# Splitting the hidden activations of an MLP group inside the up group ahead of their down products, and not during another group's down products

## The chip, the cores and the metric

The kernel runs on one core of a Trainium2 chip. The metric is the device time of one execution in microseconds (us). A core has five engines that take their instructions independently: TensorE (PE in the profile; its weight loads are PEld), VectorE (DVE), ScalarE (ACT), GpSimd (POOL) and SyncE (SP), the last of which only issues DMAs here.

## The reference

One layer of a streaming encoder on a float32 sequence of 512 frames with 1024 features:

```python
h = h + concat([fox_attention(...), hgrn2(...)]) @ w_out
h = h + memory_cross_attention(rmsnorm(h, norm_x_g), mem_n, w_xq, w_xkv, w_xo)
u = rmsnorm(h, norm_ff_g) @ w1            # w1: 1024 x 4096
h = h + jnp.square(jax.nn.relu(u)) @ w2   # w2: 4096 x 1024
return rmsnorm(h, final_norm_g)
```

The change lies in the last two products, the squared-ReLU MLP.

## The kernel before

**Precision by splitting.** TensorE multiplies in a reduced float32 format. To keep the precision, each operand is split in two: a high half (ACT copies the float32 data into the reduced format) and a low half (DVE subtracts the high half from the data). A product is then three matmuls: high by high, high by low, low by high. For weights this is `split_of` (lines 178 to 189): ACT at line 182 writes `whu` or `whd` (up or down weight), DVE at line 186 writes `wlu` or `wld`. For the hidden activations, the squared ReLU of the up products, it is `hidden_part` (lines 1491 to 1501): ACT at line 1496 writes the high half of `hb`, DVE at line 1498 or 1500 the low half. One `hb` is 128 x 512 numbers in each half.

**Groups and products.** The 4096 hidden features are cut into eight groups of 512. Groups 2 to 7 compute their up product in seven block products instead of eight (a Strassen-like scheme, `mlp_up7`), and all groups do so for the down product (`mlp_down`). The seven products are named "1", "5", "6", "2", "7", "3", "4", in the order in which TensorE does them (`PRODUCTS`). Each needs its own combination of weight blocks (some added up in DRAM ahead of time by accumulating DMAs on the POOL queue, line 446, or added into a loaded block, line 1359) and of activation blocks. The activation combinations of a group are formed by `hidden_sums` on DVE (lines 1481 to 1484) after its up products: `n6`, `s5`, `s7`, `s3`, besides plain quarters of the squared activations `sq`. In the profile, an `hb` made from a combination reads `hb<-s` (keys "5", "7", "3") or `hb<-n` (key "6"), and one made from a plain quarter `hb<-sq` (keys "1", "2", "4").

**Order of the groups.** The main loop (lines 1698 to 1707) does up group 1, and then for each further group g: up group g, `hidden_sums(g)`, down group g-1. So the sequence is up 1, down 0, up 2, down 1, ... up 6, down 5, up 7, and at the end the down products of groups 6 and 7 together, alternating. When a down group g-1 runs, the activations of group g are already there.

**Where the hb splits are written.** `hb_order` lists all keys in the order of use. `hidden_ahead(key, n)` splits the next n keys from `key` on that are not split yet and whose group has been summed. It is called

- in the up loop (line 1700), after each of the seven products of an up group, for the down group that follows. The count is 0 after the first product, then 1, 2, 3 and 4;
- in `mlp_down`, ahead of each product for its own key (line 1538), and after each product for four keys from its own on (`HB` is 4, line 1562). The four keys may reach into the next group.

In the kernel before, the calls at line 1562 after products "7", "3" and "4" of a down group thus split keys "1", "5" and "6" of the following group. In the up group between, only key "2" is left to split.

**Weights.** The seven up weights of a group are prepared in the order "1", "6", "5", "2", "7", "3", "4" (`SPLITS`), the down weights in the order of use. `unit` (lines 1374 to 1386) keeps the splits about four weights ahead of the product in hand and the loads (line 1345, on the SP queue) about eight. High and low halves rotate through four buffers each.

**Buffers.** The pool `s4` has 12 buffers of 4 KB per partition. Four hold the result rows `acc` throughout the MLP. The other eight are shared by the `hb` and by part of the raw weights (the "6" block, which is later turned into "4", and two of each five others).

**What sets the order.** TensorE's order is the program's, by hand (line 332). For ACT, DVE, POOL and SP a planner orders the instructions when the kernel is built: it runs a model of the engines, and whenever an engine is free in it, it gives it the ready instruction that comes first in program order. An instruction whose output needs a buffer is ready only when one is free in the model. Weight splits count as written 20 instructions later than they are (`ahead(PW)`, line 1353), except those of up weights "3" and "4". So a split can run well ahead of its place in the program, if an engine and a buffer are free.

In an up group, ACT also copies product "1" from bank U to bank V (line 1426), product "5" from bank Y (line 1429) and the sum with "6" from U to Y (line 1431), and does the squared ReLU (lines 1389, 1390). TensorE may go on into a bank only after such a copy out of it. In a down group DVE adds the finished products to `acc` (lines 1513, 1515).

Of the kernel before, what the change touches and what calls it, by code (L numbers as in the profile page):

```python
# [40 lines left out]
RAWS, HB, LOADS = 5, 4, 8  # L41
# [5 lines left out]
def emit(  # L47
# [69 lines left out]
    def mm(name, shape=(S,)):  # L117
        return mmp.tile([P] + list(shape), F32, tag="mm", name=name)
# [1191 lines left out]
    sqs, comb, hbs = {}, {}, {}  # L1310
# [63 lines left out]
    def unit(*key):  # L1374

        while key not in units:
            unit_q.popleft()[1]()
        got = units[key]
        at = order.index(key)
        if key[0] == "u" and key[2] in ("5", "6"):  # L1380
            at = at - 1 if key[2] == "5" else at
        while unit_q and len(order) - len(unit_q) < at + 4:
            unit_q.popleft()[1]()
        while load_q and len(order) - len(load_q) < at + LOADS:
            load_q.popleft()()
        return got
# [104 lines left out]
    def hidden_part(g, name):  # L1491

        src = comb[g][name]
        hb = s4([2, 2, HS], f"hb{g}{name}", R)
        sign = -1.0 if name == "6" else 1.0
        ac.activation(hb[:, 0], src, AF.Copy, scale=sign)  # L1496
        if name == "6":
            ve.scalar_tensor_tensor(hb[:, 1], src, -1.0, f(hb[:, 0]), op0=ALU.mult, op1=ALU.subtract)
        else:
            ve.tensor_tensor(hb[:, 1], src, f(hb[:, 0]), ALU.subtract)  # L1500
        hbs[g, name] = hb

    def hidden_ahead(key, n):

        used = hb_order.index(key)
        for k in hb_order[used : used + n]:
            if k not in hbs and k[0] in comb:
                hidden_part(*k)

    def add_to(ps, rows, half, t, sign):  # L1510
        a = acc[2 * rows + t][:, half * S : (half + 1) * S]
        if sign > 0:
            ve.tensor_tensor(a, ps, a, ALU.add)
        else:
            ve.scalar_tensor_tensor(a, ps, -1.0, a, op0=ALU.mult, op1=ALU.add)
# [11 lines left out]
    def mlp_down(gs):  # L1527

        end = gs[-1] == NG - 1
        banks = {}  # L1530
        for n, name in enumerate(PRODUCTS):
            bank, first_, goes = PLAN[name]
            if end and name == PRODUCTS[-1]:
                last_product(gs, banks)
                return
            for g, t in [(g, t) for g in gs for t in range(2)]:
                whi, wlo = unit("d", g, name)
                hidden_ahead((g, name), 1)
                hb = hbs[g, name]
                if first_ and g == gs[0]:  # L1540
                    banks[bank, t] = {"U": sc, "Y": tr}[bank](f"{bank}{g}{t}")
                ps = banks[bank, t]
                ts_ = slice(t * P, (t + 1) * P)
                for k in range(2):
                    hi, lo = hb[:, 0, k, ts_], hb[:, 1, k, ts_]
                    begin = first_ and g == gs[0] and k == 0
                    te.matmul(ps, hi, whi[:, k, :], start=begin, stop=False, skip_group_check=True)  # L1547
                    te.matmul(ps, hi, wlo[:, k, :], start=False, stop=False, skip_group_check=True)  # L1548
                    at = te.matmul(ps, lo, whi[:, k, :], start=False, stop=k == 1, skip_group_check=True)  # L1549
                presum.tick(6 * S / 2400, at)  # L1550
                if end and (g, t) == (gs[0], 1):
                    hidden_ahead((g, name), HB + 1)
                if g != gs[-1]:
                    continue
                if name == "1":
                    banks["V", t] = mm(f"V{g}{t}")
                    ac.activation(banks["V", t], ps, AF.Copy)
                for rows, half, sign in goes:
                    add_to(ps, rows, half, t, sign)
                    if end and (name, rows) in FINAL:  # L1560
                        finish(2 * rows + t, half)
            hidden_ahead((gs[-1], name), HB)
            yield

    def last_product(gs, banks):
# [68 lines left out]
    def finish(tb, half):  # L1634

        a = acc[tb]
        cs = slice(half * S, (half + 1) * S)
        if tb not in fin:
            e = sm(1, f"fe{tb}")
            ac.activation(t2(f"fj{tb}"), a[:, cs], AF.Square, scale=1.0 / 32.0, accum_out=e)  # L1640
            gp.tensor_tensor(e, e, eps3[:, tb : tb + 1], op=ALU.add)
            ag = t2(f"fa{tb}")
            gp.tensor_tensor(ag, a[:, cs], gfin[half], op=ALU.mult)
            fin[tb] = (e, cs, ag)
            return
        o = s4([D], f"fo{tb}")
        r = row_scale(squares(tb, o, cs, fin[tb][0], f"fv{tb}"), f"fr{tb}")
        if tb == 1:

            deferred.extend((tb, half, o, r))  # L1650
            return
        scale_a(tb, o, r)
        dma_a(tb, o)
        scale_b(tb, half, o, r, gfin[half])
# [43 lines left out]
    for g in range(1, NG):  # L1698
        for n, _ in enumerate(mlp_up_group(g)):
            hidden_ahead((g - 1, PRODUCTS[0]), min(n, HB))  # L1700
            if g == 1:
                next(sums, None)
                next(sums, None)
        hidden_sums(g)
        if g < NG - 1:
            for _ in mlp_down((g - 1,)):
                pass
# [4 lines left out]
    for _ in mlp_down((NG - 2, NG - 1)):  # L1712
        pass
# [28 lines left out]
```

## Time and profile before

| | |
|---|---|
| median of 3 runs | 761.94 us |
| lowest and highest | 761.64 and 762.18 us |
| the profiled execution, whole time | 762.01 us |
| its span, first to last instruction | 760.1 us |
| TensorE matmuls busy | 747.9 us (98% of the span) |
| VectorE busy | 540.1 us (71%) |
| ScalarE busy | 430.7 us (57%) |
| granted TensorE clock, mean | 0.997 |

The profile comes from one execution. Times in a timeline count from the start of the span. A line of it gives start, duration, engine, line of the kernel, operation, tile written <- tiles read, and shapes; in brackets stand the idle time of the engine just before and the instruction that ended it. Consecutive instructions overlap at their ends, so the distance between two starts can be shorter than a duration. A line of waits gives who waited for whom, the sum in us, how often, and the longest. Tile names carry no group number; which group an `hb` or a weight belongs to follows from the order. L1547 to L1549 are the three matmuls of a down product, L1420 to L1422 those of an up product.

### The profile page before, as it was taken

The page shows a single profiled execution, that of the slowest core. Times are in us where ns is not written, and L with a number is a line of the kernel's source. Part 1 is how long each engine was busy: PE and PEld are TensorE (multiplying, and loading weights), DVE is VectorE, ACT ScalarE, POOL GpSimd, SP SyncE. Part 2 cuts the span into 40 slices and gives each one's busy share as a digit, 9 for nine tenths or more (in the row PEclk, how much of TensorE's full clock was granted, in tenths as well). Part 3 has the DMA queues.
Part 4 walks back from the last instruction along what each step waited for, and adds up shares of the span by engine and source line. Part 5 has one row for each costly group of instructions (what it writes and reads, how often), then busy time and mean ns, then how long its engine had stood idle before and what let it go on. Part 6 is the DMA issues. An engine that isn't in the chain of part 4 may idle for free.

```text
span 760.1 us, 12027 instructions
## 1 busy us (share of the span) xinstructions
PE 747.9 (98%) x4501; PEld 648.8 (85%) x4501; DVE 540.1 (71%) x844; ACT 430.7 (57%) x715; POOL 197.3 (26%) x274
## 2 busy tenths in 40 slices
PE   9999999999999999999999999999999999999996
PEld 6889888888888988788888888898989889898985
DVE  5647863677778667755536658968787777878697
ACT  5655554656666533244434395667575757474873
POOL 7207431323442236621111100111111111100034
PEclk9999999999999999999999999999999999999998
DMA  8641987567946688966659849797988888967452
GB/s 248 195 118 57 321 254 230 179 226 242 329 157 217 215 189 189 193 139 137 129 131 180 182 93 269 165 267 190 235 235 208 216 240 212 233 195 225 135 112 110
DMA packets 106619, 148.17 MB, mean 195 GB/s; under 512 B 6033, under 2 KB 73146, under 8 KB 106562
## 3 DMA queue, kind: packets, MB, share of 16 engines
q1 hardware_dynamic: 83826, 109.12, 44.0%
q0 software_dynamic: 22144, 37.25, 28.0%
q10 hardware_dynamic: 592, 1.05, 0.4%
q8 instruction: 35, 0.57, 0.3%
q14 instruction: 22, 0.18, 0.1%
HBM read 143.19 MB, written 48.25 MB: 252 GB/s over the span
## 4 chain that ended last, share of the span: by engine, by line
PE 92%; DVE 3%; ACT 1%; issue 1%; DMA 1%; POOL 1%; SPq 0%; ACTq 0%; POOLq 0%
PE U L1547 4%; PE U L1548 4%; PE U L1549 4%; PE uU L1420 3%; PE uU L1421 3%; PE uU L1422 3%; PE wo L255 2%; PE xw L255 2%; PE xw L257 2%; PE xw L256 2%; PE u L257 2%; PE wo L256 2%; PE u L255 2%; PE Y L1547 2%; PE Y L1549 2%; PE Y L1548 2%
## 5 line engine op out<-in xcount | busy, mean ns | idle before, releaser
L186 DVE TENSOR_TENSOR wld<-wrd,whd 128x1024 fp32r<-128x1024 f32 x56 | 68.3, 1222 | 15.8 <-ACT whd L182 15.7
L182 ACT ACTIVATE whd<-wrd 128x1024 fp32r<-128x1024 f32 x56 | 59.1, 1055 | 17.6 <-PE uU L1421 6.8
L186 DVE TENSOR_TENSOR wlu<-wru,whu 128x1024 fp32r<-128x1024 f32 x42 | 49.7, 1218 | 24.5 <-ACT whu L182 24.5
L182 ACT ACTIVATE whu<-wru 128x1024 fp32r<-128x1024 f32 x42 | 43.6, 1054 | 25.4 <-PE U L1549 11.1
L1547 PE MATMUL U<-whd,hb 128*128 128x512 f32 x120 | 46.8, 390 | 0.0
L1548 PE MATMUL U<-wld,hb 128*128 128x512 f32 x120 | 46.8, 390 | 0.0
L1549 PE MATMUL U<-whd,hb 128*128 128x512 f32 x120 | 46.7, 389 | 0.0
L446 POOL DMA_DIRECT2D wsd<-in_w_dram x16 | 17.5, 1093 | 80.3 <-PE xw L257 18.3
L1016 POOL TENSOR_SCALAR bi<-nF,Ft 128x128 f32<-128x128 f32 (+3 forms) x32 | 21.2, 670 | 59.8 <-PE pt L1048 34.7
L446 POOL DMA_DIRECT2D wsu<-in_w_dram x12 | 14.1, 1176 | 65.9 <-PE xq L257 21.0
L1422 PE MATMUL uY<-xs_hi,wlu 128*128 128x256 f32 x96 | 27.8, 290 | 3.2 <-DVE wlu L186 3.1
L1359 POOL DMA_DIRECT2D wru<-in_w_dram x6 | 7.9, 1314 | 88.3 <-DVE wlu L186 88.3
L1359 POOL DMA_DIRECT2D wrd<-in_w_dram x8 | 9.7, 1210 | 80.0 <-DVE wld L186 63.3
L1496 ACT ACTIVATE hb<-sq 128x512 fp32r<-128x512 f32 x24 | 15.1, 631 | 24.4 <-DVE wlu L186 8.3
L1422 PE MATMUL uU<-x_hi,wlu 128*128 128x256 f32 x96 | 27.2, 283 | 0.0
L1420 PE MATMUL uU<-xs_hi,whu 128*128 128x256 f32 x96 | 27.2, 283 | 0.0
L1421 PE MATMUL uU<-xs_lo,whu 128*128 128x256 f32 x96 | 27.2, 283 | 0.0
L1422 PE MATMUL uU<-xs_hi,wlu 128*128 128x256 f32 x96 | 27.2, 283 | 0.0
L1421 PE MATMUL uU<-x_lo,whu 128*128 128x256 f32 x96 | 27.2, 283 | 0.0
L1420 PE MATMUL uY<-xs_hi,whu 128*128 128x256 f32 x96 | 27.1, 283 | 0.0
L1420 PE MATMUL uU<-x_hi,whu 128*128 128x256 f32 x96 | 27.1, 283 | 0.0
L1421 PE MATMUL uY<-xs_lo,whu 128*128 128x256 f32 x96 | 27.1, 283 | 0.0
(997 smaller groups left out, 2685.0 us busy)
## 6 DMA issues: line engine op xcount, KB each, us to landing
wsd<-in_w_dram SPq DMA_DIRECT2D x24, 512.0 KB, 5.6
wrd<-in_w_dram SPq DMA_DIRECT2D x24, 512.0 KB, 6.0
wrd<-wsd SPq DMA_DIRECT2D x24, 512.0 KB, 4.1
wsu<-in_w_dram SPq DMA_DIRECT2D x18, 512.0 KB, 7.7
wru<-in_w_dram SPq DMA_DIRECT2D x18, 512.0 KB, 7.6
wru<-wsu SPq DMA_DIRECT2D x18, 512.0 KB, 5.1
wsd<-in_w_dram POOLq DMA_DIRECT2D x16, 512.0 KB, 8.0
wsu<-in_w_dram POOLq DMA_DIRECT2D x12, 512.0 KB, 6.8
```

The lines of the kernel that those rows point to most:

```text
L182: at = ac.activation(hi, raw, AF.Copy)
L186: ve.tensor_tensor(lo, raw, f(hi), ALU.subtract)
L255: te.matmul(ps, wh, hi, start=n_ == 0 and not begun, stop=False)
L256: te.matmul(ps, wh, lo, start=False, stop=False)
L257: at = te.matmul(ps, wl, hi, start=False, stop=k == order[-1])
L446: yield gp.dma_start(wsum[kind, g, name], src, accum_op=ALU.add, **more)
L1420: te.matmul(ps[:, i, :], whi[:, k, ws], xh[:, k, :], start=begin, stop=False, skip_group_check=True)
L1421: te.matmul(ps[:, i, :], whi[:, k, ws], xl[:, k, :], start=False, stop=False, skip_group_check=True)
L1422: at = te.matmul(ps[:, i, :], wlo[:, k, ws], xh[:, k, :], start=False, stop=k == UK - 1, skip_group_check=True)
L1547: te.matmul(ps, hi, whi[:, k, :], start=begin, stop=False, skip_group_check=True)
L1548: te.matmul(ps, hi, wlo[:, k, :], start=False, stop=False, skip_group_check=True)
L1549: at = te.matmul(ps, lo, whi[:, k, :], start=False, stop=k == 1, skip_group_check=True)
```

## The change

`hidden_ahead` gets a third argument, the groups within which it may split ahead. The call behind each down product passes the groups whose down products are running, so it no longer reaches into the next group. The calls in the up loop, which pass nothing, are unchanged, and now find keys "1", "5" and "6" not yet split. They split "1" after up product "5", "5" after "6", "6" after "2", and "2" after "7". For group 6, whose keys alternate with those of group 7, they split "1" after "5" and "5" after "2". Every `hb` is computed from the same numbers as before, and none is added or left out.

```diff
-    def hidden_ahead(key, n):
+    def hidden_ahead(key, n, within=None):
 
         used = hb_order.index(key)
         for k in hb_order[used : used + n]:
-            if k not in hbs and k[0] in comb:
+            if k not in hbs and k[0] in comb and (within is None or k[0] in within):
                 hidden_part(*k)
...
-            hidden_ahead((gs[-1], name), HB)
+            hidden_ahead((gs[-1], name), HB, gs)
             yield
```

## The prediction

> **What bounds the kernel now.** I read the page first, then TensorE's waits from the start of the MLP on, then the stretches around each wait on TensorE, VectorE (DVE) and ScalarE (ACT). Two lines of the page, and the only line of the waits view of TensorE from 440 us to the end:
>
> ```profile
> span 760.1 us, 12027 instructions
> PE 747.9 (98%) x4501; PEld 648.8 (85%) x4501; DVE 540.1 (71%) x844; ACT 430.7 (57%) x715; POOL 197.3 (26%) x274
> ...
> PE uY L1422 <- DVE wlu L186: 3.1, 5, 0.7
> ```
>
> TensorE is busy nearly throughout, so only its few gaps can be won or widened. In the MLP one thing makes it wait: the low half of an up weight (wlu) for product "5", the second product of an up group. The timeline of TensorE at that place, one stretch for each up group from 2 to 7 (start, duration; in brackets the idle time before it and what ended it):
>
> ```profile
> 497.36 0.28 PE L1421 MATMUL uY<-xs_lo,whu 128*128 128x256 f32 x1
> 497.94 0.38 PE L1422 MATMUL uY<-xs_hi,wlu 128*128 128x256 f32 x1 [0.30 <-DVE wlu L186]
> 498.16 0.28 PE L1420 MATMUL uY<-xs_hi,whu 128*128 128x256 f32 x1
> 498.28 0.28 PE L1421 MATMUL uY<-xs_lo,whu 128*128 128x256 f32 x1
> ...
> 537.14 0.28 PE L1421 MATMUL uY<-xs_lo,whu 128*128 128x256 f32 x1
> 538.12 0.39 PE L1422 MATMUL uY<-xs_hi,wlu 128*128 128x256 f32 x1 [0.70 <-DVE wlu L186]
> 538.34 0.28 PE L1420 MATMUL uY<-xs_hi,whu 128*128 128x256 f32 x1
> ...
> 578.30 0.39 PE L1422 MATMUL uY<-xs_hi,wlu 128*128 128x256 f32 x1 [0.71 <-DVE wlu L186]
> ...
> 618.49 0.39 PE L1422 MATMUL uY<-xs_hi,wlu 128*128 128x256 f32 x1 [0.70 <-DVE wlu L186]
> ...
> 658.67 0.39 PE L1422 MATMUL uY<-xs_hi,wlu 128*128 128x256 f32 x1 [0.71 <-DVE wlu L186]
> ...
> 697.87 0.28 PE L1421 MATMUL uY<-xs_lo,whu 128*128 128x256 f32 x1
> 698.25 0.39 PE L1422 MATMUL uY<-xs_hi,wlu 128*128 128x256 f32 x1
> 698.47 0.28 PE L1420 MATMUL uY<-xs_hi,whu 128*128 128x256 f32 x1
> ```
>
> These matmuls normally follow each other every 0.12 us (498.16 to 498.28). From the one before the late one to the one after it should take 0.24 us. It takes 0.80 in group 2, a loss of 0.56; 1.20 in group 3, a loss of 0.96; 0.60 in group 7, a loss of 0.36. The loss is the bracketed idle time plus 0.26, so groups 4, 5 and 6 lose 0.97, 0.96 and 0.97. Together **4.78 us**, more than the 3.1 of the waits view.
>
> Why is wlu late? The DVE timeline through the end of the down group before up group 3 and into that group, the chain of waits there, and DVE's busy time by stretch (the columns of the last are stretch, length, then busy time and instructions of PE, PEld, DVE, ACT and POOL, clock, DMA share, GB/s):
>
> ```profile
> 530.38 0.68 DVE L1500 TENSOR_TENSOR hb<-sq,hb 128x512 fp32r<-128x512 f32 x1
> 530.98 1.22 DVE L186 TENSOR_TENSOR wlu<-wru,whu 128x1024 fp32r<-128x1024 f32 x1
> ...
> 533.32 0.68 DVE L1500 TENSOR_TENSOR hb<-s,hb 128x512 fp32r<-128x512 f32 x1
> 533.91 1.22 DVE L186 TENSOR_TENSOR wlu<-wru,whu 128x1024 fp32r<-128x1024 f32 x1
> 535.05 1.28 DVE L1513 TENSOR_TENSOR acc<-U,acc 128x512 f32<-128x512 f32 x2
> 536.25 0.68 DVE L1498 SCALAR_TENSOR_TENSOR hb<-n,hb 128x512 fp32r<-128x512 f32 x1
> 536.85 3.49 DVE L186 TENSOR_TENSOR wlu<-wru,whu 128x1024 fp32r<-128x1024 f32 x3
> 541.04 0.69 DVE L1500 TENSOR_TENSOR hb<-sq,hb 128x512 fp32r<-128x512 f32 x1 [0.70 <-ACT hb L1496]
> 545.58 1.23 DVE L186 TENSOR_TENSOR wlu<-wru,whu 128x1024 fp32r<-128x1024 f32 x1 [3.85 <-ACT whu L182]
> ```
>
> ```profile
> 536.33 0.60 DVE hb L1498
> 536.93 1.15 DVE wlu L186
> ```
>
> ```profile
> 517.80:534.60 16.80, 16.80 (x77) 13.97 (x76) 16.75 (x24) 10.24 (x14) 1.19 (x1) 1.00 0.77 181
> 534.60:538.10 3.50, 2.81 (x24) 2.61 (x22) 3.50 (x6) 1.81 (x3) 2.35 (x2) 1.00 0.93 323
> 538.10:545.60 7.50, 7.48 (x62) 7.48 (x63) 2.96 (x4) 3.37 (x7) 0.00 (x0) 1.00 1.07 227
> ```
>
> DVE is full without a break from 517.8 to the late wlu (16.75 of 16.80 us, then 3.50 of 3.50), then idle for more than half of 7.5 us. In its backlog stand three hb splits of the next group: hb<-sq at 530.38 ("1"), hb<-s at 533.32 ("5"), hb<-n at 536.25 ("6"). Nobody needs them before the next down group, a whole up group later. The last stands right ahead of the late wlu, and the chain that ended last runs through both.
>
> **The change part by part.** *Taken out of the down groups.* The restriction bites where the four keys ahead reach into the next group: after products "7", "3" and "4". Down groups 0 to 4 lose three hb splits each (keys "1", "5", "6"); down group 5 loses two ("1" and "5" of group 6, as the order there alternates with group 7, not computed yet). That is 17 splits, each one ACT copy and one DVE instruction; none is added or dropped, and no DMA is issued by them. On DVE one split delays what follows by 0.60 us (530.38 to 530.98; 536.25 to 536.85). In group 3 the low half now ends at 536.93 + 1.15 = 538.08; TensorE would take it at 537.14 + 0.12 = 537.26: late by 0.82. Three splits fewer bring it to 536.28, early by 0.98.
>
> It cannot come earlier than the work ahead of it allows. That is the pair of additions from bank U, the second of which needs the last down matmul:
>
> ```profile
> 533.92 0.39 PE L1549 MATMUL U<-whd,hb 128*128 128x512 f32 x1
> ```
>
> It ends at 534.31; one addition (0.68) ends near 535.0, the low half near 536.1. So the backlog, not this floor, sets 536.28. In group 2 the same step is late by 497.94 - 0.04 - 497.48 = 0.42 and gains 1.8; in group 7 by 698.21 - 697.99 = 0.22 and gains two splits, 1.2. All six gaps should close: **-4.8 us**. Bounds: 0 (nothing moves earlier) to -4.78 (there is no more TensorE idle in the MLP to take). I take the full end, since the surplus is 0.98 of 1.8 in the tightest groups.
>
> *Added to the up groups.* Up groups 2 to 6 get three more splits, 7 gets two, after products "5", "6" and "2". DVE: 3 x 0.60 = 1.8 us against 4.5 idle in 538.10 to 545.60. ACT's timeline there, and the matmul that starts product "7":
>
> ```profile
> 531.62 1.06 ACT L182 ACTIVATE whu<-wru 128x1024 fp32r<-128x1024 f32 x1 [0.62 <-PE Y L1549]
> ...
> 538.06 0.58 ACT L1426 ACTIVATE uV<-uU 128x512 f32<-128x512 f32 x1
> 540.37 0.63 ACT L1496 ACTIVATE hb<-sq 128x512 fp32r<-128x512 f32 x1 [1.73 <-DVE wlu L186]
> 541.06 0.60 ACT L1429 ACTIVATE y<-uY 128x512 f32<-128x512 f32 x1
> 544.00 0.58 ACT L1431 ACTIVATE uY<-uU 128x512 f32<-128x512 f32 x1 [2.34 <-PE uU L1422]
> ...
> 546.62 0.28 PE L1420 MATMUL uU<-xs_hi,whu 128*128 128x256 f32 x1
> ```
>
> ACT has 7.50 - 3.37 = 4.1 us idle for 3 x 0.63 = 1.9. If an hb copy falls right ahead of the copy of bank U at 544.00 it delays that by 0.63; "7" overwrites U at 546.62, and the copy is done at 544.58, 2.0 us ahead. So I cost the additions at nothing, between 0 and the rival on ACT below. The cover is these idle stretches; without it each split would cost 0.60 to 0.63.
>
> *Buffers and queues.* An hb takes one of the 12 buffers that up and down raw weights also use. In the down tail three are now free about 10 to 20 us longer. The SP queue waits for such buffers; one row of its waits from 440 us on:
>
> ```profile
> SPq L1345 <- PE Y L1549: 34.5, 7, 8.0
> ```
>
> Loads may therefore go out earlier, POOL's accumulations behind a wlu likewise by up to 1.8 us. No TensorE wait on a DMA stands in the MLP, so I count no gain, and no loss either: in the up group the same four hb of a group lie in the buffers at its end as before.
>
> *Rule against the trace.* Idle time of TensorE that repeats alike is, in the Trainium skill, "Perfetto Trace Analysis", section "Optimization Strategy", a possible sign of too few buffers; then freeing DVE would not help and the sum would be 0 instead of -4.8. The trace does not agree here: DVE was never idle ahead of the late wlu, so it did not wait for a buffer.
>
> The **sum**: the profiled execution took 762.01 us (span 760.1 and 1.9 around it), 0.07 above the median of 761.94. 762.01 - 4.8 = **757.2**. From no change a measurement of this kernel tells about 0.2%, 1.5 us.
>
> **The rivals.** *Partial, 758.6.* The planner may put an hb back early, since it fills any engine that its model holds idle. If only one split leaves the tail, 0.60 us is won: groups 3 to 6 stay 0.22 late, which costs 0.36 each as in group 7 now, 1.4 together; 757.2 + 1.4. For it: the hb at 540.37 runs ahead of "6", though it is written behind "7". Against: the late low half is written earlier than the moved hb now are, and its high half (531.62 in the ACT fence) is done at 532.7, long before DVE comes to it at 536.9.
>
> *It does nothing, 761.9.* If all three are pulled back into the down tail, or the weight's buffers are what binds, the gaps stay. Against: DVE full to the end; the weight goes ahead by program order wherever both are ready.
>
> *Slower, 770.9: ACT blocked.* At 540.37 the hb copy waited 1.73 us for a wlu to release its buffer, with the copy of bank Y behind it, since ACT takes its work in order. That DVE and ACT queues are strictly first in, first out is also what the Trainium skill says in "PSUM — Partial Sum Buffer", "Engine vs sequencer instructions"; the trace agrees at this row. If four hb copies wait like this ahead of the copy of U, the room is from 538.64 to 546.62 - 0.58 = 546.04, 7.40 us. Four times 0.63 and 0.60 for y take 3.12, which leaves 4.28 for waits. Four waits of 1.73 are 6.92: 2.64 too many, and 0.1 to restart, in five groups 13.7 us: 757.2 + 13.7. It outweighs the gain from about 1.28 us a wait on. Against: DVE reaches those wlu up to 1.8 us sooner, and three more buffers are free.
>
> **How the numbers follow.** Full closing 0.68 (757.2, own range 756.5 to 758.0), partial 0.10 (758.6), nothing 0.08 (761.9), ACT blocked or another order that the planner finds worse 0.14 (763.5 and up, 770.9 as worked out). The range has to take in the first three, which hold 0.86: from 756.5, the full closing and 0.7 for a shorter end of the kernel or the spread, to 762.2, the highest time before. Faster by over 0.2%: the first two, 0.78; same 0.08; slower 0.14.
>
> **What would show it.** Right: no TensorE wait for wlu at product "5"; no hb<-n or hb<-s of a later group on DVE ahead of the third wlu; these between that and the next wlu instead; an up and a down group together 0.96 us shorter (39.2 for the 40.18 from 538.12 to 578.30). Wrong: an hb still ahead of the late wlu on DVE; ACT waiting for a buffer at an hb with the copies of U behind it; TensorE waiting for an hb at the first down product, or for a weight's raw load.

## The result and the profile after

The changed kernel takes **756.83 us** (median of 6 runs, 756.41 to 757.07) against 761.81 (6 runs, 761.50 to 762.18): a ratio of 0.9933, 95% interval 0.9921 to 0.9946, so 5.0 us or 0.67% faster. Predicted were 757.2 us in a range from 756.5 to 762.2.

Two lines of the page of the changed kernel:

```profile
span 754.7 us, 12022 instructions
PE 746.1 (99%) x4501; PEld 648.3 (86%) x4501; DVE 540.4 (72%) x844; ACT 430.8 (57%) x715; POOL 198.8 (26%) x274
```

The instruction counts of the five engines are the same, and their busy times within 1%; only the span is clearly shorter. The waits view of TensorE from 440 us on, which had one line before, is now empty. The TensorE timeline at the start of product "5" of up group 3:

```profile
536.00 0.28 PE L1421 MATMUL uY<-xs_lo,whu 128*128 128x256 f32 x1
536.12 0.28 PE L1422 MATMUL uY<-xs_hi,wlu 128*128 128x256 f32 x1
536.24 0.28 PE L1420 MATMUL uY<-xs_hi,whu 128*128 128x256 f32 x1
```

The matmuls run through at their 0.12 us, where the late one had come 0.98 us behind its forerunner. VectorE's timeline of the same stretch, the end of down group 1 and the start of up group 3:

```profile
529.25 1.21 DVE L186 TENSOR_TENSOR wlu<-wru,whu 128x1024 fp32r<-128x1024 f32 x1
530.38 1.28 DVE L1515 SCALAR_TENSOR_TENSOR acc<-Y,acc 128x512 f32<-128x512 f32 x2
531.58 1.21 DVE L186 TENSOR_TENSOR wlu<-wru,whu 128x1024 fp32r<-128x1024 f32 x1
532.71 1.28 DVE L1513 TENSOR_TENSOR acc<-U,acc 128x512 f32<-128x512 f32 x2
533.91 2.35 DVE L186 TENSOR_TENSOR wlu<-wru,whu 128x1024 fp32r<-128x1024 f32 x2
536.18 0.68 DVE L1500 TENSOR_TENSOR hb<-sq,hb 128x512 fp32r<-128x512 f32 x1
537.05 1.23 DVE L186 TENSOR_TENSOR wlu<-wru,whu 128x1024 fp32r<-128x1024 f32 x1 [0.19 <-ACT whu L182]
538.19 0.68 DVE L1500 TENSOR_TENSOR hb<-s,hb 128x512 fp32r<-128x512 f32 x1
538.79 0.68 DVE L1498 SCALAR_TENSOR_TENSOR hb<-n,hb 128x512 fp32r<-128x512 f32 x1
539.40 0.68 DVE L1500 TENSOR_TENSOR hb<-sq,hb 128x512 fp32r<-128x512 f32 x1
543.48 2.36 DVE L186 TENSOR_TENSOR wlu<-wru,whu 128x1024 fp32r<-128x1024 f32 x2 [3.40 <-ACT whu L182]
```

The weights and additions of the down tail follow each other with no hb between them. The third wlu, the one that was late, starts at 533.91 and, at 1.22 us, ends near 535.13; TensorE takes it at 536.12. With the 0.04 us that lay between the end of the weight and the matmul in the kernel before (538.08 and 538.12), it is about 0.95 us early where it had been late. The three hb now stand behind it, and behind them and the hb of key "2" (539.40) VectorE is idle for 3.40 us.

ScalarE's timeline of the same stretch shows something else:

```profile
528.73 0.61 ACT L1496 ACTIVATE hb<-sq 128x512 fp32r<-128x512 f32 x1
529.25 0.62 ACT L1496 ACTIVATE hb<-s 128x512 fp32r<-128x512 f32 x1
530.49 1.07 ACT L182 ACTIVATE whu<-wru 128x1024 fp32r<-128x1024 f32 x1 [0.62 <-PE Y L1549]
531.45 0.61 ACT L1496 ACTIVATE hb<-n 128x512 fp32r<-128x512 f32 x1
533.21 1.06 ACT L182 ACTIVATE whu<-wru 128x1024 fp32r<-128x1024 f32 x1 [1.14 <-PE U L1549]
```

The high halves of the three hb are still copied during the other group's down products: the planner pulled them forward into ScalarE's idle time. Only their low halves on VectorE moved behind the weights. An hb takes its buffer with the high half, so the buffers are held nearly as long as before too: counted from the first matmul of the up group, they are taken 3.7, 1.5 and 2.2 us later than in the kernel before. So little is left by which ScalarE or the buffers could have made the gain; the experiments below test both.

From the first matmul of up group 2 to the last product of the kernel (L1578, bank U) the kernel before took 748.22 - 494.37 = 253.85 us by these rows of its chain and of its TensorE timeline, the changed one 742.87 - 493.79 = 249.08:

```profile
494.37 0.28 PE L1420 MATMUL uU<-x_hi,whu 128*128 128x256 f32 x1
748.22 2.72 PE U L1578 x12
```

```profile
493.79 0.28 PE L1420 MATMUL uU<-x_hi,whu 128*128 128x256 f32 x1
742.87 2.72 PE U L1578 x12
```

That is 4.77 us less, against 4.78 worked out gap by gap. The spans differ by 5.4; the other 0.6 lies ahead of the changed part, where the two profiled executions already stand 0.58 apart at the start of up group 2. This start moves between 493.79 and 494.79 us in the profiles of the nine kernels of this document. From the first down product to it all nine take the same 19.04 us, so the difference arises ahead of the down groups, where the programs are the same.

### The profile page after: what moved, and what is told of

It reads as the page before. It is cut to its first block, busy times and chain, and to the rows that moved or that the text cites. A ratio compares the mean times of both kernels' runs of the same rounds, so it can differ in the third digit from the quotient of the medians.

```text
span 754.7 us, 12022 instructions
## 1 busy us (share of the span) xinstructions
PE 746.1 (99%) x4501; PEld 648.3 (86%) x4501; DVE 540.4 (72%) x844; ACT 430.8 (57%) x715; POOL 198.8 (26%) x274
## 4 chain that ended last, share of the span: by engine, by line
PE 94%; DVE 2%; ACT 1%; issue 1%; POOL 1%; ACTq 0%; POOLq 0%
PE U L1547 4%; PE U L1548 4%; PE U L1549 4%; PE uU L1422 3%; PE uU L1421 3%; PE uU L1420 3%; PE wo L255 2%; PE xw L257 2%; PE xw L256 2%; PE xw L255 2%; PE u L255 2%; PE u L256 2%; PE Y L1547 2%; PE Y L1549 2%; PE Y L1548 2%; PE wo L256 2%
## 5 line engine op out<-in xcount | busy, mean ns | idle before, releaser
L1159 ACT ACTIVATE x_hi<-hT,gv 128x512 fp32r<-128x512 f32 x16 | 11.4, 715 | 27.5 <-DVE hT L1158 27.4
```

## The experiments

The theory: what counts is VectorE's backlog, that is how much work stands on it ahead of wlu of product "5". The rivals: the buffers that an hb holds through the up group, ScalarE's load in the down groups, or only the one hb right ahead of the weight. All times below are medians; the kernel before ran beside them, at 761.73 us with e1, e2, e3 and e6 and at 761.74 with the three e5.

| kernel | hb or unused work ahead of the late wlu | us | ratio to before, 95% interval |
|---|---|---|---|
| before | 3 hb | 761.81 | |
| changed | 0 | 756.83 | 0.9933 (0.9921 to 0.9946) |
| e2_two | 1 hb | 756.89 | 0.9938 (0.9926 to 0.9951) |
| e1_one | 2 hb | 758.41 | 0.9957 (0.9943 to 0.9970) |
| e3_u5first | 2 hb, and 2 additions fewer | 757.31 | 0.9941 (0.9929 to 0.9954) |
| e5_dummy2 | 1 unused | 756.62 | 0.9935 (0.9923 to 0.9948) |
| e5_dummy3 | 2 unused | 758.88 | 0.9964 (0.9950 to 0.9977) |
| e5_dummy4 | 3 unused | 762.26 | 1.0007 (0.9998 to 1.0016) |
| e6_pinned | 0, hb on ScalarE late too | 756.77 | 0.9936 (0.9924 to 0.9949) |

**Part of the change: only key "6" kept out.**

```diff
-            hidden_ahead((gs[-1], name), HB, gs)
+            hidden_ahead((gs[-1], name), HB, gs if name == "4" else None)
```

> Only the split of key 6 is kept out of the down groups; keys 1 and 5 of the next group are split there again, and on VectorE two hb stand ahead of the late weight (one for group 7). Theory (VectorE's backlog ahead of wlu of product 5; in the changed kernel that weight is about 0.95 us early, each hb ahead of it takes 0.60): 2 x 0.60 - 0.95 = 0.25 late, a gap of some 0.36 to 0.4 us in each of up groups 3 to 6 and none in 2 and 7, so 756.8 + 1.5 = 758.3 us. Rival (buffers: the gap comes from hb that hold shared buffers through the up group): two of three are held as before, so about two thirds of the 5.0 us come back, 760.1 us. Rival (it is the last hb alone, right ahead of the weight, that matters): 756.8 us, no gap.

Measured 758.41 us. The TensorE waits view from 440 us on has no line here either, and yet the gaps are there. VectorE's timeline has two hb of the next group (530.09 and 533.02) ahead of the third wlu:

```profile
530.09 0.68 DVE L1500 TENSOR_TENSOR hb<-sq,hb 128x512 fp32r<-128x512 f32 x1
530.69 1.22 DVE L186 TENSOR_TENSOR wlu<-wru,whu 128x1024 fp32r<-128x1024 f32 x1
531.82 1.28 DVE L1515 SCALAR_TENSOR_TENSOR acc<-Y,acc 128x512 f32<-128x512 f32 x2
533.02 0.68 DVE L1500 TENSOR_TENSOR hb<-s,hb 128x512 fp32r<-128x512 f32 x1
533.62 1.22 DVE L186 TENSOR_TENSOR wlu<-wru,whu 128x1024 fp32r<-128x1024 f32 x1
534.76 1.28 DVE L1513 TENSOR_TENSOR acc<-U,acc 128x512 f32<-128x512 f32 x2
535.96 3.49 DVE L186 TENSOR_TENSOR wlu<-wru,whu 128x1024 fp32r<-128x1024 f32 x3
```

TensorE's timeline there:

```profile
536.84 0.28 PE L1421 MATMUL uY<-xs_lo,whu 128*128 128x256 f32 x1
537.23 0.39 PE L1422 MATMUL uY<-xs_hi,wlu 128*128 128x256 f32 x1
537.45 0.28 PE L1420 MATMUL uY<-xs_hi,whu 128*128 128x256 f32 x1
```

From start to start, the late matmul follows its forerunner after 0.38 or 0.39 us in groups 3 to 6, and the next follows after 0.22, in place of 0.24 together: 0.36 to 0.37 lost in each of four groups, 1.5 us, and no gap in groups 2 and 7. The measured step over the changed kernel is 1.6. The last hb alone is not the cause, since it is gone here.

**Keys "5" and "6" kept out.**

```diff
-            hidden_ahead((gs[-1], name), HB, gs)
+            hidden_ahead((gs[-1], name), HB, None if name == "7" else gs)
```

> Keys 5 and 6 are kept out of the down groups; only key 1 of the next group is split there, one hb ahead of the late weight on VectorE. Theory (backlog): 0.60 is less than the 0.95 in hand, so no gap of TensorE and 756.8 us, the same as the changed kernel. Rival (buffers): one of three hb held as before, a third of the 5.0 us back, 758.5 us.

Measured 756.89 us, and no matmul of bank Y longer than the normal 283 ns, so no gap. One hb fits into the time in hand, two do not. The buffer theory asked for 758.5. But neither e1_one nor e2_two says much on the buffers: in both, as in the changed kernel, ScalarE copies the high halves of all three hb before the up group starts, so all three buffers are taken there. The kernels that follow test the buffers.

**The kernel before, with only the weight of product "5" moved up on VectorE.**

```diff
-            with ahead(0 if late else PW):
+            with ahead(0 if late or (kind == "u" and part == "5") else PW):
```

> The kernel before, with all three hb split during the other group's down products as there; only the split of up weight 5 is no longer written 20 instructions later than it is. On VectorE that weight then runs ahead of the last two additions and of the hb of key 6; the hb hold their buffers as long as before. Theory (VectorE's order): 1.2 + 0.6 = 1.8 us earlier, from 0.82 late to 0.98 early, no gap, 757.0 us. Rival (buffers, or ScalarE relieved in the down group): nothing of that is changed, 761.8 us.

Measured 757.31 us. VectorE's timeline:

```profile
533.19 0.68 DVE L1500 TENSOR_TENSOR hb<-s,hb 128x512 fp32r<-128x512 f32 x1
533.79 2.35 DVE L186 TENSOR_TENSOR wlu<-wru,whu 128x1024 fp32r<-128x1024 f32 x2
536.06 1.28 DVE L1513 TENSOR_TENSOR acc<-U,acc 128x512 f32<-128x512 f32 x2
537.26 0.68 DVE L1498 SCALAR_TENSOR_TENSOR hb<-n,hb 128x512 fp32r<-128x512 f32 x1
```

ScalarE copies all three hb during the other group's down products, at the same times before the up group as in the kernel before, so they hold their buffers through the up group as there. But the second wlu of the pair at 533.79 is the weight of "5", ahead of the additions and of hb<-n. (The first is that of "6": POOL's addition into the block of "6", which waits for its split, starts at 535.30, 0.3 us after the first of the pair ends at 535.00. In the kernel before it started at 535.43, as long after the end of the wlu at 533.91.) The gaps are gone. So neither the buffers nor ScalarE's load made them. That 757.31 is 0.48 above the changed kernel is not a remnant of the gaps: from the first matmul of up group 2 to the end of the last matmul, the profiles of e3_u5first, e2_two, e5_dummy2 and e6_pinned take 254.67 us, as the changed kernel does.

**Work put back on VectorE alone.** To the changed kernel, two, three or four subtractions whose result nobody uses are added per down group. The last of them stands behind the late weight, the others ahead of it. They take nothing of ScalarE and no shared buffer. The edit of the last of the three; the other two differ only in the names:

```diff
             hidden_ahead((gs[-1], name), HB, gs)
+            if not end and name in "2734":   # "34" in e5_dummy2, "734" in e5_dummy3
+                rows, half, sign = goes[0]
+                src = acc[2 * rows + 1][:, half * S : (half + 1) * S]
+                ve.tensor_tensor(rbc, src, src, ALU.subtract)
```

> The changed kernel, with one more VectorE subtraction of 128x512 numbers (its result is used by nobody) after each of products 3 and 4 of a down group; on VectorE the first stands ahead of the late weight, the second behind it. It uses no buffer of the shared pool and nothing of ScalarE. Theory (backlog): one dose of 0.60 against 0.95 in hand, no gap, 756.8 us. Rival (any added work in the down group costs, as VectorE is full there): about 0.6 us in each of six groups, 760.4 us.

> The same after products 7, 3 and 4: two unused subtractions stand ahead of the late weight on VectorE, one behind it. Theory (backlog): 1.20 - 0.95 = 0.25 late, a gap that costs 0.36 to 0.4 us in each of up groups 3 to 7 and none in group 2, 756.8 + 2.0 = 758.8 us. Rival (buffers, ScalarE): neither is touched, 756.8 us.

> The same after products 2, 7, 3 and 4: three unused subtractions stand ahead of the late weight on VectorE, as many as the hb that the change took away. Theory (backlog): 1.80 - 0.95 = 0.85 late, about 1.0 us in each of up groups 3 to 7 and some 0.6 in group 2, 5.5 us, 762.3 us: the gaps of the kernel before are back, and group 7 has a full one. Rival (buffers, ScalarE): neither is touched, 756.8 us.

Measured 756.62, 758.88 and 762.26 us: nothing, then 2.0, then 5.4 us over the changed kernel. With three ahead of the weight, VectorE and TensorE look as in the kernel before, with unused work in the place of the hb. VectorE's timeline and the waits view of TensorE of e5_dummy4:

```profile
527.57 0.69 DVE L1566 TENSOR_TENSOR rbc<-acc 128x512 f32<-128x512 f32 x1
...
531.64 0.68 DVE L1566 TENSOR_TENSOR rbc<-acc 128x512 f32<-128x512 f32 x1
532.25 1.28 DVE L1515 SCALAR_TENSOR_TENSOR acc<-Y,acc 128x512 f32<-128x512 f32 x2
533.45 1.21 DVE L186 TENSOR_TENSOR wlu<-wru,whu 128x1024 fp32r<-128x1024 f32 x1
534.58 0.68 DVE L1566 TENSOR_TENSOR rbc<-acc 128x512 f32<-128x512 f32 x1
535.18 1.28 DVE L1513 TENSOR_TENSOR acc<-U,acc 128x512 f32<-128x512 f32 x2
536.38 1.22 DVE L186 TENSOR_TENSOR wlu<-wru,whu 128x1024 fp32r<-128x1024 f32 x1
```

```profile
PE uY L1422 <- DVE wlu L186: 3.9, 6, 0.7
```

The late wlu ends near 537.6, and the timeline of TensorE in e5_dummy4 has the gap again, as long as before:

```profile
536.66 0.28 PE L1421 MATMUL uY<-xs_lo,whu 128*128 128x256 f32 x1
537.65 0.39 PE L1422 MATMUL uY<-xs_hi,wlu 128*128 128x256 f32 x1 [0.71 <-DVE wlu L186]
537.87 0.28 PE L1420 MATMUL uY<-xs_hi,whu 128*128 128x256 f32 x1
```

There are six waits in the view in place of five, since group 7 now has three pieces of work ahead of its weight and a full gap; that is why this kernel is no faster than the one before, though it has the change.

**The hb held back on ScalarE too.** In the up groups the four copies are written later, and an order-only dependency ties each behind the copy of bank U to Y:

```diff
+    late_in = [0]
...
-        ac.activation(hb[:, 0], src, AF.Copy, scale=sign)
+        split = ac.activation(hb[:, 0], src, AF.Copy, scale=sign)
+        if 2 <= late_in[0] < NG:
+            order_only = mybir.DependencyInfo(mybir.DependencyClass.NoSync, mybir.DependencyReason.DATA)
+            tc.add_manual_dep(split.ins, copyY[late_in[0]].ins.name, order_only, reason="in the up group")
...
-            hidden_ahead((g - 1, PRODUCTS[0]), min(n, HB))
+            late_in[0] = g if g in SEVEN else 0
+            hidden_ahead((g - 1, PRODUCTS[0]), min(n, HB) if g not in SEVEN or n > 2 else 0)
+            late_in[0] = 0
```

> The changed kernel, with the four hb copies of the following down group tied on ScalarE behind the copy of bank U to Y, so that none can be pulled forward into the down group (in the changed kernel ScalarE still does three of them there). Theory: the copies find idle time in the up group on ScalarE too, no gap, 756.8 us. Rival (the up group has no room on ScalarE: the squares or the weight splits behind them come late): a TensorE gap in the second half of the up group or at the first down products, slower than 757.5 us.

Measured 756.77 us. ScalarE's timeline in up group 3 (its line 1498 is the hb copy, line 1496 elsewhere):

```profile
542.11 0.58 ACT L1431 ACTIVATE uY<-uU 128x512 f32<-128x512 f32 x1 [2.34 <-PE uU L1422]
542.61 2.00 ACT L182 ACTIVATE whu<-wru 128x1024 fp32r<-128x1024 f32 x2
544.51 0.62 ACT L1498 ACTIVATE hb<-sq 128x512 fp32r<-128x512 f32 x1
545.02 0.59 ACT L1389 ACTIVATE sq<-uV 128x512 f32<-128x512 f32 x1
545.50 0.62 ACT L1498 ACTIVATE hb<-s 128x512 fp32r<-128x512 f32 x1
546.02 0.62 ACT L1390 ACTIVATE sq<-sq 128x512 f32<-128x512 f32 x1
546.55 0.62 ACT L1498 ACTIVATE hb<-n 128x512 fp32r<-128x512 f32 x1
```

Here the copies really are in the up group, between the squares, in its busier half, and TensorE has no wait. Whether ScalarE does them early or late makes no difference. Nor does the time at which the buffers are taken: in this kernel alone the three hb take theirs only in the up group, about 15 us later than in the changed kernel, and the time is the same.

No run was faster than the changed kernel beyond the spread. From up group 2 on, neither the waits view nor the distances between the starts of neighbouring up and down matmuls show a gap of TensorE in the changed kernel that is left to take.

## Why the prediction was right, point by point

- **The loss.** Six gaps of 4.78 us together were forecast to go, and 4.77 us went; one up and one down group together now take 39.22 us, where 39.2 was forecast. The median of 756.83 lies 0.4 below the forecast 757.2. About half of that is the starting point, a profiled execution 0.2 above the median of the kernel before; the other half lies outside the stretch that was worked out, and no run here says what makes it.
- **The cause.** A VectorE without a pause ahead of the late weight, and 0.60 us for each hb in it. The prediction had 0.98 us in hand after the change; the trace shows about 0.95. Doses of one, two and three bear that out: 0.60 is hidden (756.89 and 756.62), 1.20 is a quarter of a microsecond too much (758.41 and 758.88), 1.80 brings everything back (762.26).
- **The signs.** There is no wait for wlu at product "5", and no hb of a later group ahead of the third wlu on VectorE. One detail was off: hb<-s and hb<-n were expected between that wlu and the next, and stand two weights further back, after the fifth.
- **The partial rival** (one split leaves the tail) was given 758.6 us; e1_one, which is that case, took 758.41.
- **Nothing changes, by buffers.** e3_u5first closes the gaps with the buffers held as before, and e6_pinned takes the buffers much later and gains nothing more, so these repeated gaps did not come from too few buffers.
- **ScalarE blocked.** It did not happen. In the changed kernel the hb copy of key "2" waits 0.80 us for its buffer, in place of the 1.73 of before, and e6_pinned shows room for all four copies even in the second half. The row at 540.37, from which the prediction worked this rival out, shows a wait but no harm: the last matmul into bank Y (below, kernel before) ends near 541.02, and the copy of Y starts at 541.06, so the hb copy, done at 541.00, did not hold it up. For the same reason this row cannot show whether ScalarE takes its work strictly in order.

```profile
540.74 0.28 PE L1422 MATMUL uY<-xs_hi,wlu 128*128 128x256 f32 x1
```

- **Where the prediction's picture was off.** It put the added ScalarE work into the up groups' idle time. The planner left three of the four copies in the down groups. That cost nothing, since the sum had counted the copies at nothing either way. With the copies the buffers stayed in the down groups: they are free 1.5 to 3.7 us longer, not about 10 to 20.
- **Buffers and queues.** Loads move on SP (that of a down weight goes out at 525.04 us, in the kernel before at 531.62), but TensorE shows no wait for them, as assumed.

## What to carry to other kernels

An engine that is 71% busy over the kernel can still be the bound for some 20 us at a time (VectorE from 517.8 to 538.1 us), and what then matters is the order of its queue: look at what stands ahead of the instruction that the bottleneck waits for, and when each of these is needed. Work that is needed later is moved behind it, or the needed one ahead; both gave the same here. How much it is worth follows from a deadline: what stays below the time in hand costs nothing, and what goes beyond it costs in full, here with about 0.1 us on top at each gap (0.25 late lost 0.36 to 0.37, 0.82 late lost 0.96).

## What the runs showed that was not expected

The waits view leaves out small gaps of TensorE. The prediction had met this in group 7; in e1_one and e5_dummy3 it goes as far as no line at all in the MLP, though 0.36 to 0.37 us are lost in each of four and five groups. The end of a matmul is modelled at 0.28 us where the next normally starts after 0.12, so most of such a gap does not show as idle time: of the step of 0.39 us in e1_one only some 0.1 is left, and the view does not list it. Distances between starts show the whole.
